# Band attention on one core: which engine multiplies the 384- and 512-column probability rows by their inverse sums

## The chip, the cores and the metric

The kernel runs on one core of a Trainium2 chip. The metric is the time of one execution on the device, in microseconds (us); lower is better. A core has a matrix engine (TensorE, in the profile PE, with its weight loads as PEld), three engines for elementwise work (VectorE or DVE, ScalarE or ACT, GpSimd or POOL), and DMA queues; SyncE (SP) issues most of the loads. Each engine works through its own queue in a fixed order, and waits at an instruction whose inputs or buffers are not ready.

## The reference, cut to what matters

The kernel computes a small encoder trunk of two layers on 512 tokens of width 1024, in float32. The first layer mixes tokens by a matrix memory (mLSTM), the second by attention over a band of chunks; both add an attention over 256 memory tokens, and each is followed by a gated channel mixer with a short convolution. The change lies in the band attention of the second layer:

```python
def band_attention(q, k_pad, v_pad, rel_table):
    # chunk c (64 tokens) attends to keys of chunks c-8..c; 12 heads of width 64
    ...
    bias = rel_table.astype(jnp.float32)[:, idx]
    scale = B_HEAD_DIM ** -0.5

    def one_chunk(c):
        ...
        s = jnp.einsum('bqhd,bkhd->bhqk', qc, kc).astype(jnp.float32) * scale + bias
        valid = (start - KV_PAD + kj) >= 0
        s = jnp.where(valid, s, -jnp.inf)
        p = jax.nn.softmax(s, axis=-1).astype(vc.dtype)
        return jnp.einsum('bhqk,bkhd->bqhd', p, vc)
```

With 512 tokens the band holds every earlier chunk, so that a block of 128 queries with number T (0 to 3) sees the first (T + 1) x 128 keys: 128, 256, 384 or 512 columns.

## The kernel before, in words

Activations lie with features on the 128 partitions and tokens along the columns. Float32 products are made from a high and a low part of each operand: the helper `split` (lines 146 to 151) casts the source to the high part on ScalarE (line 147) and subtracts it on VectorE to get the low part (line 148), and `mm3` (lines 203 to 205) adds three matmuls, high by high, high by low, low by high.

The second mixer goes over six pairs of heads (j = 0 to 5). `project_pair(j)` makes keys, values and queries of a pair with TensorE, eight steps of `mm3` a projection, and evacuates them on VectorE (lines 1480, 652) and ScalarE (`head_queries` and `head_keys`, lines 600 to 613). `band_attention(j, ...)` is the attention of the pair. Its generator `softmax(T)` does for both heads h of the pair:

- scores of 128 queries against (T + 1) x 128 keys on TensorE (line 622), into a PSUM bank of the group `sc` (three banks);
- line 1518, VectorE: adds the bias, negates, and keeps the row's smallest value `mn`; the result `e` goes to SBUF and frees the bank;
- line 1522, ScalarE: the exponential, with the row's sum `sm` as a second result (a short extra instruction reads it out);
- line 1523, VectorE: `sm` becomes its reciprocal;
- line 1524, VectorE: `e` is multiplied by `sm`, one scalar for each partition. This is the line that changes.

`transposed(T)` then turns `e` over on TensorE in blocks of 128 x 128 (line 1533, T + 1 blocks into one bank of the group `tr`, which has two), and `split` takes the bank to the high and the low probabilities in `pt` (ScalarE's cast 147, then VectorE's subtraction 148, which frees the bank). The program writes them in the order softmax 0, softmax 1, transposed 0, softmax 2, transposed 1, softmax 3, transposed 2, transposed 3; then the products with the values (lines 1554 and 1555) and their evacuation (`values`, lines 641 and 642). Rows of line 1524 are buffers of the group `t`, eight in all, and `sm` comes from a rotating set of small buffers.

What sets the order of the work: `weave` (lines 1566 to 1583) puts a fixed number of `mm3` steps of other work, projections of later pairs or parts of the output projection, behind each step of the attention, so that TensorE has matmuls while the elementwise engines work. In this stage no engine's order is written by hand: the framework that lays out the instructions takes the program's order as a priority and issues to each engine, by its own estimate of when inputs and buffers are ready, what comes first. The queues so made are fixed in the program. (In the channel mixers and at the beginning, the order of TensorE, ScalarE and VectorE is written by hand.) Weights come through SyncE's queue into three buffers `wr`, from which `split` makes `wh` and `wl`; the bias rows come through GpSimd's queue (line 1508).

The memory attention of the same mixer (line 679 for the exponential, 682 for the multiplication) has a code of its own and is not touched.

Of the kernel before, what the change touches and what calls it, by code (L numbers as in the profile page):

```python
# [12 lines left out]
AF = mybir.ActivationFunctionType  # L13
ALU = mybir.AluOpType
# [45 lines left out]
def trunk(  # L60
# [19 lines left out]
    V, A, G = nc.vector, nc.scalar, nc.gpsimd  # L80
# [14 lines left out]
    def sb(tag, shape, dtype=F32):  # L95
        count[0] += 1
        return pool.tile(shape, dtype, tag=tag, name=f"{tag}{count[0]}", bufs=bufs[tag])

    def ps(tag):
        count[0] += 1  # L100
        return psum.tile([P, S], F32, tag=tag, name=f"p{tag}{count[0]}", bufs=pbufs[tag])
# [6 lines left out]
    def small(n=4, dtype=F32):  # L108
        smalls[0] += 1
        i = smalls[0] % 26  # L110
        return sb("s0" if i < 6 else "s1" if i < 12 else "s2", [P, 16], dtype)[:, :n]
# [34 lines left out]
    def split(hi, lo, src, on_act=True, pinned=False):  # L146
        high = A.copy(hi, src) if on_act else V.tensor_copy(hi, src)  # L147
        low = V.tensor_tensor(out=lo, in0=src, in1=f(hi), op=ALU.subtract)  # L148
        if pinned:
            pin(high)  # L150
            pin(low)
# [485 lines left out]
    def values(outs):  # L637

        s, t = sb("t", [P, S]), sb("t", [P, S])
        for o, r in zip(outs, HEADS):  # L640
            A.copy(t[r, :], o[HD:, :])
            V.tensor_tensor(out=s[r, :], in0=o[:HD, :], in1=t[r, :], op=ALU.add)
        hi, lo = sb("u", [P, S], F32R), sb("u", [P, S], F32R)
        split(hi, lo, s)
        return hi, lo
# [9 lines left out]
    def scores(outs, q, tsl, k, c):  # L655

        for h in range(2):
            head_scores(outs[h], h, q, tsl, k, c, True)
# [537 lines left out]
    e, u, c, r = (cpool.tile([P, TT, AH], F32, name=f"gate{i}") for i in range(4))  # L1196
# [270 lines left out]
    def hi_at(pt, s, T, n=1):  # L1467
        return pt[:, s * 640 + (T + 1) * P : s * 640 + (T + 1 + n) * P]

    def lo_at(pt, s, T, n=1):  # L1470
        return pt[:, (3 - s) * 640 + (T - s) * P : (3 - s) * 640 + (T - s + n) * P]

    def blocks(pt, o, step, n):
        a = pt[:, o : o + P]
        return bass.AP(tensor=a.tensor, offset=a.offset, ap=[list(a.ap[0]), [step, n], [1, P]])
# [25 lines left out]
    def band_attention(j, q, k, v):  # L1501
        pts = [sb("pt", [P, 5 * S], F32R) for _ in range(2)]
        biases = []
        for h in range(2):
            rep = reps[2 * j + h]
            biases.append(sb("bias", [P, S]))
            src = bass.AP(tensor=rep.tensor, offset=rep.offset + P - 1, ap=[[RW - 1, P], [1, S]])
            tc.keep_in_program_order(G.dma_start(biases[h], src))
        es = {}

        def softmax(T):
            n = (T + 1) * P
            ss = [ps("sc")[:, :n] for _ in range(2)]
            scores(ss, q, slice(T * P, n), k, slice(0, n))
            for h in range(2):
                e = sb("t", [P, S])[:, :n]
                mn, sm = small(1), small(1)
                V.tensor_tensor_reduce(
                    out=e, in0=ss[h], in1=biases[h][:, S - n :], scale=-1.0, scalar=BIG,
                    op0=ALU.add, op1=ALU.min, accum_out=mn,  # L1520
                )
                A.activation(e, e, AF.Exp, bias=mn, scale=-1.0, accum_out=sm)
                V.reciprocal(sm, sm)
                V.tensor_scalar(e, e, sm, None, op0=ALU.mult)
                es[T, h] = e
            yield

        def transposed(T):
            n = (T + 1) * P
            for h in range(2):  # L1530
                tp = ps("tr")
                for b in range(T + 1):
                    nc.tensor.transpose(tp[:, b * P : (b + 1) * P], es[T, h][:, b * P : (b + 1) * P], ident)  # L1533
                split(
                    blocks(pts[h], (T + 1) * P, 640, T + 1), blocks(pts[h], 3 * 640 + T * P, -768, T + 1),
                    tp[:, :n].rearrange("p (b t) -> p b t", t=P),
                )
            yield

        yield from softmax(0)  # L1540
        yield from softmax(1)
        yield from transposed(0)
        yield from softmax(2)
        yield from transposed(1)
        yield from softmax(3)
        yield from transposed(2)
        yield from transposed(3)
        outs = []
        for h in range(2):
            o2 = ps("tr")  # L1550
            outs.append(o2)
            for s in range(TT):
                w = v[s][:, h, :]
                nc.tensor.matmul(o2[:, s * P :], w, hi_at(pts[h], s, s, TT - s), start=s == 0, stop=False)  # L1554
                nc.tensor.matmul(o2[:, s * P :], w, lo_at(pts[h], s, s, TT - s), start=False, stop=s == TT - 1)  # L1555
            yield
        mixes[j] = values(outs)
# [220 lines left out]
```

## Time and profile before

| | us |
|---|---|
| median of 3 runs | 1168.01 |
| lowest and highest | 1167.87 and 1168.32 |
| the profiled execution | 1168.55 |
| its span, first to last instruction | 1166.5 |
| granted TensorE clock, mean | 0.998 of full speed |

How to read the profile: busy times are of one execution, in us, and means of single instructions in ns. A row of a group names the line of the kernel, the engine, the operation, what it writes and reads (`t<-t,s` is from a row and a column of scalars to a row), the shapes, the count, the busy time and mean, and behind the second bar the engine's idle time just before such instructions with what ended it. "A <- B: 1.3, 4, 0.4" in the view of waits means that A waited for B 1.3 us in total, 4 times, 0.4 at the longest. A timeline row is start (us), duration (us), engine, line, operation; what stands in brackets is the idle time before it and what ended it. Matmuls are pipelined, and a matmul's row is longer than the distance to the next one.

### The profile page before, as it was taken

How to read it: one execution, taken by the hardware profiler on the slowest of the kernel's cores; microseconds unless marked ns; L12 is line 12 of the kernel's file. 1: busy time of each engine (PE TensorE's matmuls, PEld its weight loads, DVE VectorE, ACT ScalarE, POOL GpSimd, SP SyncE). 2: the span in 40 equal slices, each digit the busy share in tenths (PEclk: the TensorE clock that was granted, in tenths of full speed). 3: DMA queues.
4: the chain of work that ended last, by engine and by line, in shares of the span. 5: the costliest groups of instructions: out<-in, count | busy, mean ns of one | idle time of the engine just before them, and what ended most of it. 6: DMA issues, size and time to landing. Idle time of an engine off the chain costs nothing.

```text
span 1166.5 us, 19282 instructions
## 1 busy us (share of the span) xinstructions
PE 1156.2 (99%) x7189; PEld 1033.2 (89%) x7189; DVE 1001.8 (86%) x1781; ACT 747.9 (64%) x1343; POOL 151.2 (13%) x254
## 2 busy tenths in 40 slices
PE   9999999999999999999999999999999999999997
PEld 9988888888999999999888888778899999999986
DVE  6877688779999988888797888898999998889977
ACT  6548677657776655555575667776776665555654
POOL 1211101000122222111021000100010111111100
PEclk9999999999999999999999999999999999999999
DMA  8745325244468878777564322335445767777682
GB/s 282 230 110 134 96 56 153 66 134 140 139 157 182 213 178 195 182 173 162 147 193 133 91 62 63 122 107 157 142 126 143 174 146 180 172 180 174 143 157 78
DMA packets 207855, 171.26 MB, mean 147 GB/s; under 512 B 9256, under 2 KB 182030, under 8 KB 207762
## 3 DMA queue, kind: packets, MB, share of 16 engines
q1 hardware_dynamic: 188018, 123.93, 37.1%
q0 software_dynamic: 19168, 45.06, 19.3%
q8 instruction: 56, 0.92, 0.3%
q10 hardware_dynamic: 576, 1.05, 0.2%
q14 instruction: 37, 0.30, 0.1%
HBM read 133.09 MB, written 40.85 MB: 149 GB/s over the span
## 4 chain that ended last, share of the span: by engine, by line
PE 96%; DVE 2%; ACT 1%; DMA 0%; issue 0%; POOL 0%; POOLq 0%; DVEq 0%
PE pmm L203 19%; PE pmm L204 18%; PE pmm L205 18%; PE ptr L204 6%; PE ptr L203 6%; PE ptr L205 6%; PE psc L203 5%; PE psc L204 5%; PE psc L205 5%; PE psc L622 2%; PE ptr L1533 1%; PE ptr L1554 1%; PE ptr L1555 1%; PE ptr L691 1%; PE pmm L513 0%; PE ptr L705 0%
## 5 line engine op out<-in xcount | busy, mean ns | idle before, releaser
L203 PE MATMUL pmm<-u,wh 128*128 128x256 f32 (+1 forms) x992 | 334.9, 338 | 0.1
L205 PE MATMUL pmm<-u,wl 128*128 128x256 f32 (+1 forms) x992 | 332.1, 335 | 0.0
L204 PE MATMUL pmm<-u,wh 128*128 128x256 f32 (+1 forms) x992 | 331.9, 335 | 0.0
L148 DVE TENSOR_TENSOR wl<-wr,wh 128x1024 fp32r<-128x1024 f32 (+4 forms) x165 | 184.8, 1120 | 56.0 <-ACT wh L147 55.4
L205 PEld LDWEIGHTS pmm<-u,wl 128*128 128x128 f32 x992 | 186.3, 188 | 18.9
L203 PEld LDWEIGHTS pmm<-u,wh 128*128 128x128 f32 x992 | 186.4, 188 | 16.7 <-ACT u L147 0.9
L204 PEld LDWEIGHTS pmm<-u,wh 128*128 128x128 f32 x992 | 186.5, 188 | 16.2 <-DVE u L148 0.5
L147 ACT CAST wh<-wr 128x1024 fp32r<-128x1024 f32 (+4 forms) x165 | 159.6, 970 | 62.5 <-PE pmm L204 30.1
L203 PE MATMUL ptr<-u,wh 128*128 128x512 f32 x272 | 106.5, 392 | 0.0
L204 PE MATMUL ptr<-u,wh 128*128 128x512 f32 x272 | 106.3, 391 | 0.0
L205 PE MATMUL ptr<-u,wl 128*128 128x512 f32 x272 | 105.8, 389 | 0.0
L147 ACT CAST fh<-pt 128x512 fp32r<-128x512 f32 x120 | 74.8, 625 | 34.5 <-DVE pt L1059 33.2
L203 PE MATMUL pmm<-u,fh 128*128 128x256 f32 x320 | 88.8, 278 | 0.0
L205 PE MATMUL pmm<-u,fl 128*128 128x256 f32 x320 | 88.6, 277 | 0.0
L204 PE MATMUL pmm<-u,fh 128*128 128x256 f32 x320 | 88.5, 276 | 0.0
L981 ACT COPY t<-pmm 128x256 f32<-128x256 f32 x120 | 45.0, 375 | 67.3 <-PE pmm L205 67.2
L148 DVE TENSOR_TENSOR fl<-pt,fh 128x512 fp32r<-128x512 f32 x120 | 82.3, 687 | 3.1
L765 DVE SCALAR_TENSOR_TENSOR t<-t,cols,t 128x511 f32<-128x511 f32 x88 | 65.9, 749 | 7.3 <-ACT t L772 5.8
L203 PE MATMUL psc<-u,wh 128*128 128x256 f32 (+1 forms) x208 | 63.2, 304 | 0.0
L205 PE MATMUL psc<-u,wl 128*128 128x256 f32 (+1 forms) x208 | 62.9, 302 | 0.0
L204 PE MATMUL psc<-u,wh 128*128 128x256 f32 (+1 forms) x208 | 62.9, 302 | 0.0
L203 PEld LDWEIGHTS pmm<-u,fh 128*128 128x128 f32 x320 | 60.1, 188 | 2.2 <-ACT t L981 0.7
(359 smaller groups left out, 2642.0 us busy)
## 6 DMA issues: line engine op xcount, KB each, us to landing
wr<-in_ffn_w_up_dram SPq DMA_DIRECT2D x46, 512.0 KB, 8.5
pt<-in_ffn_w_up_dram SPq DMA_DIRECT2D x40, 512.0 KB, 8.3
wr<-in_ffn_w_down_dram SPq DMA_DIRECT2D x32, 512.0 KB, 5.4
wr<-in_a_w_in_dram SPq DMA_DIRECT2D x20, 512.0 KB, 3.8
xspill<-bias POOLq DMA_DIRECT2D x32, 256.0 KB, 7.0
without_row<-bias POOLq DMA_DIRECT2D x24, 256.0 KB, 4.1
wr<-in_w_kv_dram SPq DMA_DIRECT2D x12, 512.0 KB, 4.0
without_row<-t POOLq DMA_DIRECT2D x24, 256.0 KB, 4.1
```

The source lines that it names most:

```text
L147: high = A.copy(hi, src) if on_act else V.tensor_copy(hi, src)
L148: low = V.tensor_tensor(out=lo, in0=src, in1=f(hi), op=ALU.subtract)
L203: nc.tensor.matmul(o, lh, rh, start=first, stop=False, skip_group_check=more)
L204: nc.tensor.matmul(o, lh, rl, start=False, stop=False, skip_group_check=more)
L205: nc.tensor.matmul(o, ll, rh, start=False, stop=last, skip_group_check=more)
L622: nc.tensor.matmul(o, a, b, start=first and i == 0, stop=i == 1)
L691: nc.tensor.transpose(tp[:, a, i, :], es[T2, h][:, i, a * P : (a + 1) * P], ident)
L765: V.scalar_tensor_tensor(acc[:, n:], src[:, : S - n], self.fw[:, c * FT + j : c * FT + j + 1], acc[:, n:], op0=ALU.mult, op1=ALU.add,)
L981: A.copy(o, r[:, :H])
L1533: nc.tensor.transpose(tp[:, b * P : (b + 1) * P], es[T, h][:, b * P : (b + 1) * P], ident)
L1554: nc.tensor.matmul(o2[:, s * P :], w, hi_at(pts[h], s, s, TT - s), start=s == 0, stop=False)
L1555: nc.tensor.matmul(o2[:, s * P :], w, lo_at(pts[h], s, s, TT - s), start=False, stop=s == TT - 1)
```

## The change

The multiplication of line 1524 is done by ScalarE for query blocks 2 and 3 (rows of 384 and 512 columns), as a copy with a scale for each partition; blocks 0 and 1 stay on VectorE. That concerns 2 blocks x 2 heads x 6 pairs = 24 of the 48 instructions. Nothing else is edited.

```diff
                 A.activation(e, e, AF.Exp, bias=mn, scale=-1.0, accum_out=sm)
                 V.reciprocal(sm, sm)
-                V.tensor_scalar(e, e, sm, None, op0=ALU.mult)
+                if T < 2:
+                    V.tensor_scalar(e, e, sm, None, op0=ALU.mult)
+                else:
+                    A.activation(e, e, AF.Copy, scale=sm)
                 es[T, h] = e
             yield
```

## The prediction, on record before the changed kernel ran

> **What bounds the kernel now.** I read the page first, then the table of busy time by stretch for the six band heads, the waits of TensorE, the groups with shapes kept apart, and last the timeline of two heads. The page says which engine the time belongs to.
>
> ```profile
> span 1166.5 us, 19282 instructions
> PE 1156.2 (99%) x7189; PEld 1033.2 (89%) x7189; DVE 1001.8 (86%) x1781; ACT 747.9 (64%) x1343; POOL 151.2 (13%) x254
> PE 96%; DVE 2%; ACT 1%; DMA 0%; issue 0%; POOL 0%; POOLq 0%; DVEq 0%
> ```
>
> The chain that ended last is TensorE for 96% of the span, VectorE for 2%, ScalarE for 1%. The profiled execution took 1168.55 us, 2.05 us more than its span of 1166.5; the median of the runs, 1168.01, lies 0.54 us below it. I work out a change against the profiled execution and put it on the median. A difference under 0.2% (2.34 us) is about what a measurement of this kernel cannot tell from nothing.
>
> The changed line 1524 runs only in the band attention of the second mixer.
>
> ```profile
> L1524 DVE TENSOR_SCALAR t<-t,s x48: 280/382/602, 630.3 to 795.1; 128x128 f32<-128x128 f32 x12, 128x256 f32<-128x256 f32 x12, 128x384 f32<-128x384 f32 x12, 128x512 f32<-128x512 f32 x12
> ```
>
> Its 48 instructions (shortest, median and longest in ns; first and last start in us) start between 630.3 and 795.1 us, twelve of each width, in six bursts, one for each pair of heads ("head pair" below). This is the table by stretch for the six bursts (length; busy PE, weight loads, VectorE, ScalarE, GpSimd; clock; DMA), and behind it a stretch of the output projection, in which matmuls of 512 columns follow one another without a wait.
>
> ```profile
> 629.00:642.00 13.00, 12.89 (x72) 10.76 (x71) 11.74 (x42) 8.54 (x26) 2.19 (x4) 1.00 0.42 113
> ...
> 752.00:770.00 18.00, 17.67 (x95) 14.35 (x94) 16.69 (x51) 14.12 (x36) 1.09 (x2) 1.00 0.26 68
> ...
> sum 93.00, PE 92.56 PEld 76.61 DVE 82.42 ACT 65.86 POOL 6.62; mean PE 15.43 PEld 12.77 DVE 13.74 ACT 10.98 POOL 1.10
> 820.00:840.00 20.00, 20.00 (x90) 16.52 (x89) 19.61 (x35) 15.34 (x24) 1.08 (x2) 1.00 0.53 159
> ```
>
> In the 93.00 us of the bursts TensorE is idle for 0.44 us. VectorE is busy 82.42 us of them (89%), ScalarE 65.86 (71%). So there is little time to win, and VectorE is the nearer of the two helpers to holding TensorE up. Weight loads are busy for 76.61 of 93.00 us (82%); in the projection's stretch, where TensorE is never idle, they are at 16.52 of 20.00 (83%). The bursts are about as tightly packed as that stretch.
>
> The Trainium skill, page "Perfetto Trace Analysis", section "Identifying the Most-Contended Engine", holds matmul busy time for a bad measure, and tells the reader to judge headroom by weight-load busy time. By that rule alone 16.4 us of the bursts could still be won; the trace disagrees on the headroom, since a stretch without any wait shows the same share.
>
> The waits of TensorE and of its weight loads from 612 to 832 us give the ceiling of a gain (us in total, times, longest).
>
> ```profile
> PE psc L622 <- DVE s L1518: 0.3, 1, 0.3
> ...
> PEld ptr L1533 <- DVE pt L148: 1.3, 4, 0.4
> PEld ptr L1554 <- DVE pt L148: 1.0, 4, 0.3
> ...
> PEld psc L622 <- DVE s L1518: 0.6, 1, 0.6
> PEld ptr L705 <- DVE pt L148: 0.6, 3, 0.2
> ```
>
> The largest waits that VectorE ends are 1.3 (transposes of the rows, waiting for a bank that the subtraction of the split frees), 1.0 and 0.6 (products that wait for the low half), and 0.6 (scores that wait for a bank): 3.5 us. None names line 1524, and the view of that line lists nobody who waited for it.
>
> **The change part by part.** These are the groups of the exponential (1522) and of the multiplication that moves (1524), by shape, and the nearest thing to the new instruction: line 351, ScalarE's scaling by a column.
>
> ```profile
> L1522 ACT ACTIVATE t<-t,s 128x512 f32<-128x512 f32 x12 | 8.7, 724 | 3.3 <-DVE s L1518 3.3
> L1522 ACT ACTIVATE t<-t,s 128x384 f32<-128x384 f32 x12 | 7.4, 615 | 3.6 <-DVE s L1518 3.6
> L351 ACT ACTIVATE u<-fl,cols 128x512 fp32r<-128x512 f32 x4 | 2.9, 714 | 0.0
> L1524 DVE TENSOR_SCALAR t<-t,s 128x512 f32<-128x512 f32 x12 | 5.8, 481 | 0.1
> L1524 DVE TENSOR_SCALAR t<-t,s 128x384 f32<-128x384 f32 x12 | 5.2, 432 | 0.1
> ```
>
> *Removed from VectorE:* 12 x 0.481 + 12 x 0.432 = 10.96 us. In the bursts its load falls from 82.42 to 71.46 of 93.00 us (77%). *Added to ScalarE:* 0.714 us for 512 columns by line 351; for 384 I take off what the exponential loses between the shapes, 0.724 - 0.615 = 0.109, so 0.605 us. That is 12 x 0.714 + 12 x 0.605 = 15.83 us, and ScalarE rises from 65.86 to 81.69 us (88%). The two engines change places: the busier helper was at 89% and will be at 88%. Neither amount is on the path as such, because TensorE sets the end; what counts is the rows at which TensorE has to wait. No DMA is added or moved. The transfers that these engines release (weights after the split, the bias rows after line 1518) may start a little earlier or later; no wait of TensorE above names one, so I cost that at nothing.
>
> *What VectorE's relief is worth.* Here is the end of the first head pair.
>
> ```profile
> 640.08 0.84 ACT L147 CAST pt<-ptr 128x384 fp32r<-128x384 f32 x2
> 640.21 0.16 DVE L1523 RECIPROCAL s<-s 128x1 f32<-128x1 f32 x1 [0.28 <-ACT t L1522]
> 640.41 0.49 DVE L1524 TENSOR_SCALAR t<-t,s 128x512 f32<-128x512 f32 x1
> 640.81 1.01 DVE L148 TENSOR_TENSOR pt<-ptr,pt 128x384 fp32r<-128x384 f32 x2
> 641.41 0.88 PEld L1533 LDWEIGHTS ptr<-ident,t 128*128 128x128 f32 x8 [0.43 <-DVE pt L148]
> ```
>
> A moved multiplication of 0.49 us stands on VectorE right ahead of the subtractions whose end lets the transposes go on, 0.43 us late. With it gone the subtractions could start as soon as the cast ahead of them is done, and the 0.43 us is the most that this place gives. What is late next is that cast: if the new scaling of the other head goes ahead of it on ScalarE, the cast starts up to 0.71 us later and the gain is gone. For all such places the bounds are 0 and -3.5 us (the rows above); I take -0.4, this place alone, because it is the only one that I saw with a moved instruction directly in front.
>
> *What the longer row costs.* Each moved row becomes ready later by 0.714 - 0.481 = 0.233 us (512 columns) or 0.605 - 0.432 = 0.173 us (384), and by any time that ScalarE is not free. If nothing hid it, the sum would be 12 x 0.233 + 12 x 0.173 = 4.87 us. The cover is the time between a row's end and its first transpose. The tightest place I found is the last row of the second head pair.
>
> ```profile
> 665.75 1.06 ACT L147 CAST wh<-wr 128x1024 fp32r<-128x1024 f32 x1
> 666.08 0.15 DVE L1523 RECIPROCAL s<-s 128x1 f32<-128x1 f32 x1
> 666.60 0.48 DVE L1524 TENSOR_SCALAR t<-t,s 128x512 f32<-128x512 f32 x1
> 667.20 0.31 PEld L1533 LDWEIGHTS ptr<-ident,t 128*128 128x128 f32 x3 [0.33 <-PE ptr L1533]
> ```
>
> The reciprocal is done at 666.23, the row at 667.08, the transposes load at 667.20: a cover of 0.12 us. ScalarE is in a weight cast until 666.81, so the row would be done at 666.81 + 0.714 = 667.52, 0.44 us later than now, and TensorE would be late by 0.44 - 0.12 = 0.32 us. That is the price I take for rows whose cover is too short; the bounds are 0 and +4.87.
>
> *The new wait.* Before, the multiplication stood behind its reciprocal on one engine. Now ScalarE waits for VectorE's reciprocal, and behind that waiting instruction are queued the casts of the transposed blocks, the weight casts, and the exponentials of the next rows. The transposes wait for the casts through the two banks they use. ScalarE has waits already that such a one may sit inside:
>
> ```profile
> ACT wh L147 <- PE pmm L204: 13.7, 10, 3.2
> ACT t L1522 <- DVE s L1518: 12.5, 17, 1.9
> ACT pt L147 <- PE ptr L1533: 10.3, 17, 2.1
> ```
>
> That is 13.7 + 12.5 + 10.3 = 36.5 us of ScalarE's idle time in the whole stage, over twice the 15.83 us that it gets. This is the cover, and it is why I leave the rest at nothing.
>
> The sum: -0.4 + 0.32 = -0.08 us. From 1168.55 that makes 1168.47 for a profiled execution, and about 1167.9 for the median.
>
> **The rivals.** *VectorE's backlog was what held TensorE* (faster). For it: 89% in the bursts, and the 3.5 us of waits all end with VectorE. Against it: most of them end with the subtraction of a split, which itself waits for ScalarE's cast, and ScalarE gets fuller. To show, over 2.34 of the 3.5 us must go; with 2.8 gone (four fifths) the time is 1168.01 - 2.8 = 1165.2.
>
> *ScalarE's queue holds up the casts* (slower). The place is the end of a head pair: two exponentials of 512 columns, two new scalings and the casts of the rows before are on ScalarE together, and a scaling stands in front of a cast that frees a bank. It decides from 2.34/24 = 0.10 us per moved row that no cover takes; with no cover at all the time is 1168.01 + 4.87 = 1172.9. For it: the load of 88%, and the short cover in the second head pair. Against it: the 36.5 us of waits. The Trainium skill, page "ScalarE: Activation LUTs", section "Rules for kernel authors", says that plain multiplications belong on VectorE and not on ScalarE, and so speaks for this rival; the trace agrees on the single instruction, 714 ns against 481.
>
> *The order of the queues changes more than the costs.* No order is written by hand in this stage; the framework lays the queues out by its own estimates, and another engine for 24 instructions can shift where the transposes stand among the projections' matmuls. The bursts show what a worse order is worth: TensorE idles 0.33 us in the stretch from 752 to 770 and 0.11 in the first. All six like the worst would be 6 x 0.33 - 0.44 = +1.54 us, 1169.6; all idle time gone -0.44, 1167.6. Both lie within 0.2%.
>
> *The change does not do what it says*, for instance by a load of activation tables around each copy. Line 351 is the same operation with a column as its scale, and the whole stage has a single load, behind the last row:
>
> ```profile
> L283 ACT ACT_TABLE_LOAD  x1: 1283/1283/1283, 801.9 to 801.9; - x1
> ```
>
> I give it 1 in 100, inside "slower".
>
> **How the numbers follow.** No measurable change 0.62: my sum at -0.08 us, with the bounds from reordering inside it. Faster 0.16: the backlog rival, which needs two thirds of all waits and loses to a fuller ScalarE. Slower 0.22: larger than faster, because its bound of 4.87 us is wider than 3.5 and new waits have no ceiling in the rows. The forecast is 1167.9. The range has to keep 8 in 10: its lower end goes to the backlog rival's 1165.2, its upper end to two thirds of the uncovered price, 1168.01 + 3.25 = 1171.3; about 1 in 10 is left out on each side.
>
> **What would show it.** Right: in the changed profile line 1524 keeps 24 instructions on VectorE, and the new line has 24 on ScalarE at about 0.605 and 0.714 us; VectorE loses near 11 us and ScalarE gains near 16 over the span; TensorE's idle time in the six bursts stays below 2 us. Wrong toward faster: the waits of lines 1533, 1554 and 622 for VectorE shrink to under 1.2 us and the stage ends over 2 us sooner. Wrong toward slower: waits of the transposes for ScalarE (the new scaling, or the casts of line 147) appear with over 2 us in total. A shift of the stages outside 612 to 832 us would mean that I looked in the wrong place.

## The result, and the profile after

The changed kernel takes 1180.01 us (median of 4 runs, 1179.72 to 1180.40); the kernel before, run beside it, 1168.16. The ratio is 1.0101, with a 95% interval of 1.0085 to 1.0117: 11.85 us slower, where the forecast was 1167.9 and the upper end of its range 1171.3. In all that follows a loss is counted against the runs of the kernel before that were made beside that kernel; their median was 1168.16 to 1168.52.

First the page of the changed kernel: span, busy time by engine, chain of waits.

```profile
span 1178.0 us, 19285 instructions
...
PE 1159.9 (98%) x7189; PEld 1033.2 (88%) x7189; DVE 994.3 (84%) x1757; ACT 760.4 (65%) x1367; POOL 150.9 (13%) x254
...
PE 92%; DVE 3%; ACT 3%; DMA 1%; issue 1%; SPq 0%; POOL 0%; DVEq 0%; POOLq 0%; ACTq 0%
```

The span is 11.5 us longer, with the same 7189 matmuls. TensorE's share of the chain went from 96% to 92%, and what it lost stands mostly with VectorE, ScalarE and a DMA. The moved work itself is what it should be. This is the view of the new line 1527 (count; shortest, median, longest ns; first and last start; then who waited for it):

```profile
L1527 ACT ACTIVATE t<-t,s x24: 601/666/729, 637.4 to 798.1; 128x384 f32<-128x384 f32 x12, 128x512 f32<-128x512 f32 x12
...
  PEld ptr L1536: 0.9, 4
```

The transposes (1533 before, 1536 now: the change adds three lines) wait for it 0.9 us in all. That is not where 11.85 us went. The waits of TensorE from 612 to 840 us (total us, times, longest) say where:

```profile
PEld pmm L203 <- ACT wh L147: 5.2, 1, 5.2
PE pmm L203 <- DVE rb L298: 4.7, 1, 4.7
PEld pmm L205 <- DVE wl L148: 2.6, 1, 2.6
PEld ptr L1557 <- DVE pt L148: 2.2, 5, 0.6
PE pmm L205 <- DVE wl L148: 1.9, 1, 1.9
```

Two single waits, of 5.2 and 2.6 us on the weight side (4.7 and 1.9 are the same stops, seen by the matmuls), outweigh the rest. They belong to `mm3` (lines 203 to 205) and to the split of a *weight* (147, 148), not to the attention. The table by stretch puts them behind the last head pair; before, then after (length; busy PE, weight loads, VectorE, ScalarE, GpSimd; clock; DMA share; GB/s):

```profile
800.00:840.00 40.00, 40.00 (x178) 33.06 (x177) 37.68 (x61) 29.80 (x45) 4.33 (x8) 1.00 0.60 183
```

```profile
800.00:840.00 40.00, 32.87 (x138) 25.87 (x137) 29.01 (x44) 21.36 (x33) 4.33 (x8) 0.91 0.56 169
```

Before, TensorE has no idle time here; after, 7.13 us of it, and a clock of 0.91. TensorE, VectorE and ScalarE all do less in these 40 us, so none of them is the new bound: they wait for one another. The place is the end of the out-projection, `OutProjection.finish` (lines 728 to 741). Its first five column tiles were computed among the attention; three, numbers 5 to 7, are left, and their weights are still to be split. This is TensorE's timeline there, first before, then after (start, duration, operation; in brackets the idle time before it and what ended it):

```profile
808.57 0.39 PE L203 MATMUL pmm<-u,wh 128*128 128x512 f32 x1
808.80 0.39 PE L204 MATMUL pmm<-u,wh 128*128 128x512 f32 x1
809.02 0.39 PE L205 MATMUL pmm<-u,wl 128*128 128x512 f32 x1
809.25 0.39 PE L203 MATMUL pmm<-u,wh 128*128 128x512 f32 x1
```

```profile
811.19 0.47 PE L203 MATMUL pmm<-u,wh 128*128 128x512 f32 x1 [0.49 <-DVE fh L736]
811.50 0.40 PE L204 MATMUL pmm<-u,wh 128*128 128x512 f32 x1
811.79 0.47 PE L203 MATMUL pmm<-u,wh 128*128 128x512 f32 x1
812.10 0.40 PE L204 MATMUL pmm<-u,wh 128*128 128x512 f32 x1
817.23 0.80 PE L203 MATMUL pmm<-u,wh 128*128 128x512 f32 x1 [4.73 <-DVE rb L298]
817.82 0.63 PE L204 MATMUL pmm<-u,wh 128*128 128x512 f32 x1
820.35 0.79 PE L205 MATMUL pmm<-u,wl 128*128 128x512 f32 x1 [1.90 <-DVE wl L148]
820.94 0.63 PE L203 MATMUL pmm<-u,wh 128*128 128x512 f32 x1
```

The reader is to see the order. Before, column tile 5 goes high, high, low, and on. After, the first two products of tile 5, then of tile 6, then of tile 7 come first, and only then tile 5's product with the low weights (205). So TensorE cannot go on with tile 5 until the weights of tile 7 have been cast. These are VectorE's and ScalarE's rows of the same place after the change:

```profile
810.37 1.88 DVE L736 TENSOR_TENSOR fh<-fh,pmm 128x512 f32<-128x512 f32 x3
812.16 0.68 DVE L736 TENSOR_TENSOR fh<-fh,psc 128x512 f32<-128x512 f32 x1
...
818.41 0.75 DVE L352 SCALAR_TENSOR_TENSOR u<-fl,cols,u 128x512 fp32r<-128x512 f32 x1
819.08 3.49 DVE L148 TENSOR_TENSOR wl<-wr,wh 128x1024 fp32r<-128x1024 f32 x3
```

```profile
809.15 1.05 ACT L147 CAST wh<-wr 128x1024 fp32r<-128x1024 f32 x1 [0.98 <-PE pmm L204]
...
816.15 1.03 ACT L147 CAST wh<-wr 128x1024 fp32r<-128x1024 f32 x1
```

The third cast ends at 817.18, and TensorE's 4.73 us end at 817.23. (The timeline names VectorE's norm sum, line 298, as the releaser of that matmul; its weight load, in the list of waits, names the cast. In e10 below the two come apart: the cast ends at 814.18 and that norm sum at 814.90, and the same matmul starts at 814.24.) The three subtractions that make the low weights stand behind all five residual sums and the norm work, and the first lands after 820. Before, the first of them stood right behind the first sum:

```profile
806.05 0.69 DVE L736 TENSOR_TENSOR fh<-fh,pmm 128x512 f32<-128x512 f32 x1
806.65 1.22 DVE L148 TENSOR_TENSOR wl<-wr,wh 128x1024 fp32r<-128x1024 f32 x1
```

and the third cast was done at 812.18:

```profile
811.14 1.04 ACT L147 CAST wh<-wr 128x1024 fp32r<-128x1024 f32 x1
```

Nothing in the edited lines asks for that. Counted matmul by matmul (each against the one of the same number in the old trace), TensorE is 2.62 us behind the old trace at 811.19, 7.75 at 817.23, 10.42 at 820.35 and 11.93 at 823.45, and stays there. So 9.3 us are lost in 12 us of time: 5.1 at the cast, 2.3 at the low weights, and 1.9 in matmuls that run slowly after the stop. The order of SyncE's queue changed too. Before, then after:

```profile
798.35 0.37 SPq L864 DMA_DIRECT2D pt<-in_ffn_w_up_dram  x1
798.77 1.22 SPq L869 DMA_DIRECT2D pt<-in_ffn_w_up_dram  x2
804.13 0.37 SPq L162 DMA_DIRECT2D wr<-in_b_w_out_dram  x1
```

```profile
801.31 0.37 SPq L162 DMA_DIRECT2D wr<-in_b_w_out_dram  x1
801.87 0.44 SPq L864 DMA_DIRECT2D pt<-in_ffn_w_up_dram  x1
802.36 2.38 SPq L869 DMA_DIRECT2D pt<-in_ffn_w_up_dram  x2
```

The load for column tile 7 went ahead of the three loads of the channel mixer's up-projection, on which VectorE's line 1059 waits, and with it what is queued behind that line.

### The profile page after: what moved, and what is told of

It reads as the page before. It is cut to its first block, busy times and chain, and to the rows that moved or that the text cites. A ratio compares the mean times of both kernels' runs of the same rounds, so it can differ in the third digit from the quotient of the medians.

```text
span 1178.0 us, 19285 instructions
## 1 busy us (share of the span) xinstructions
PE 1159.9 (98%) x7189; PEld 1033.2 (88%) x7189; DVE 994.3 (84%) x1757; ACT 760.4 (65%) x1367; POOL 150.9 (13%) x254
## 4 chain that ended last, share of the span: by engine, by line
PE 92%; DVE 3%; ACT 3%; DMA 1%; issue 1%; SPq 0%; POOL 0%; DVEq 0%; POOLq 0%; ACTq 0%
PE pmm L203 18%; PE pmm L205 18%; PE pmm L204 18%; PE ptr L204 6%; PE ptr L203 6%; PE ptr L205 6%; PE psc L203 5%; PE psc L204 5%; PE psc L205 5%; PE psc L622 2%; PE ptr L1536 1%; ACT t L1522 1%; PE ptr L691 1%; PE ptr L1557 1%; PE ptr L1558 1%; DMA pt<-in_ffn_w_up_dram 1%
## 5 line engine op out<-in xcount | busy, mean ns | idle before, releaser
L148 DVE TENSOR_TENSOR u<-t,u 128x512 fp32r<-128x512 f32 x78 | 55.8, 719 | 9.0 <-ACT u L147 8.4
```

## The experiments

Theory: the framework, having other costs for 24 instructions, laid the queues out differently, and the new order at the finish costs the time. Rival: the moved work itself costs it, by ScalarE's queue or the longer rows. Eight of the twelve kernels have the program of one kernel and the order of another, written as dependencies that fix only the order within a queue (four lists: TensorE, ScalarE, VectorE, SyncE, from the second mixer to the finish). Fixing an order costs next to nothing by itself: from 620 to 808 us, where e10, e11 and e12 have the work and the order of the kernel before, TensorE moves by less than 0.1 us against it. The edit:

```diff
+    ins = {i.name: i for i in nc.cur_bb.bb.instructions}
+    for ids in ORDER:
+        for a, b in zip(ids, ids[1:]):
+            dep = mybir.DependencyInfo(mybir.DependencyClass.NoSync, mybir.DependencyReason.DATA)
+            tc.add_manual_dep(ins[f"I-{b}"], f"I-{a}", dep, reason="order")
```

The expectations call their theories A, B, A1 and so on, each for itself.

**e1_new_work_old_order.** The changed kernel, ORDER the four queues of the kernel before.

> The 24 multiplications are on ScalarE as in the changed kernel, but from the first place to the last at which the two kernels' queues differ, the queues of TensorE, ScalarE, VectorE and SyncE are fixed to the order of the kernel before (each moved instruction stands in ScalarE's queue where ScalarE was at the end of its reciprocal). Theory A (the framework's new order of the queues costs the time, above all at the end of the output projection, and the work that moved costs little): 1168 to 1171 us. Theory B (the work on ScalarE makes the rows and all behind them late, whatever the order): 1178 to 1181 us.

Measured: 1173.06 us, ratio 1.0039 (1.0024 to 1.0054), +4.5 us, which is above theory A's 1171: the work costs more than expected in an order not made for it. The loss at the finish is gone: TensorE is 4.7 us late when the attention ends and 4.8 at the end of the span. What remains was lost at the rows; since this trace is 0.9 us early at 620 us, before the first row, its rows lose 5.6 us. Both places that the prediction priced can be read here, since all else stands as it stood. The first head pair's transposes, which had waited 0.43 us at 641.41:

```profile
640.49 0.42 PEld L1536 LDWEIGHTS ptr<-ident,t 128*128 128x128 f32 x4 [0.39 <-DVE pt L148]
641.48 0.42 PEld L1536 LDWEIGHTS ptr<-ident,t 128*128 128x128 f32 x4 [0.57 <-DVE pt L148]
```

The 0.43 us was not saved but became 0.39 and 0.57, because two scalings now stand ahead of the casts on ScalarE. And the second head pair's last row:

```profile
667.02 0.72 ACT L1527 ACTIVATE t<-t,s 128x512 f32<-128x512 f32 x1
```

```profile
667.79 0.42 PEld L1536 LDWEIGHTS ptr<-ident,t 128*128 128x128 f32 x4 [1.24 <-ACT t L1527]
```

There the wait grew from 0.33 to 1.24 us: the scaling waits behind the weight cast, as foreseen, but that cast also ends 0.3 us later, having another scaling ahead of it.

**e2_old_work_new_order.** The kernel before, ORDER the four queues of the changed kernel.

> All 48 multiplications stay on VectorE, each moved one right behind its reciprocal, but the four queues are fixed to the order of the changed kernel. Theory A: 1177 to 1181 us, with TensorE waiting between 808 and 825 us as in the changed kernel. Theory B: 1167 to 1170 us.

Measured: 1180.70 us, 1.0106 (1.0091 to 1.0121), +12.2 us. The whole loss, without one moved instruction, and at the same matmuls:

```profile
817.83 0.79 PE L203 MATMUL pmm<-u,wh 128*128 128x512 f32 x1 [4.73 <-DVE rb L298]
...
820.95 0.80 PE L205 MATMUL pmm<-u,wl 128*128 128x512 f32 x1 [1.90 <-DVE wl L148]
```

So the order is enough, and the rival falls as the main cause.

**e3_pair_4_alone and e4_all_but_pair_4.** Which of the moved instructions turn the layout? Only the four of pair j = 4, or only the other 20:

```diff
-                if T < 2:
+                if T < 2 or j != 4:
```

```diff
-                if T < 2:
+                if T < 2 or j == 4:
```

> Only the fifth head pair (j = 4) scales its 384- and 512-column rows on ScalarE: 4 instructions of 24, and the framework plans freely. It gives the queues at the end of the output projection the same order as in the changed kernel. Theory A: 1176 to 1179 us (the loss at the end of the projection, without the small losses in the other pairs). Theory B: a sixth of the loss, 1170 us.

> The five other head pairs (20 of 24 instructions) scale on ScalarE, the fifth as before; the framework plans freely and gives the end of the output projection the order of the kernel before, but for two VectorE instructions. Theory A: 1168 to 1171 us. Theory B: five sixths of the loss, 1178 us.

Measured: 1178.50 us, 1.0083 (1.0066 to 1.0100), +10.0 us for four instructions; and 1169.42 us, 1.0007 (0.9998 to 1.0016), +0.9 us for the other 20, which is not told apart from nothing. In e3 TensorE has the new order at the finish, in e4 the old; ScalarE and VectorE follow, but for a few instructions. Twenty moved rows cost next to nothing, four cost 10 us: the loss does not grow with the work moved.

**e7_all_rows.** All 48 rows on ScalarE.

```diff
-                if T < 2:
+                if T < 0:
```

> All 48 multiplications go to ScalarE, those of 128 and 256 columns too, twice as many as in the change; the framework plans freely, and gives the end of the projection the order of the kernel before but for two VectorE instructions. Theory A: 1169 to 1174 us, faster than the change although more work moves. Theory B: 1182 us or more.

Measured: 1171.44 us, 1.0027 (1.0017 to 1.0036), +3.1 us. Twice the moved work is 8.7 us cheaper than the change, since with it TensorE's finish comes out in the old order.

**e5_old_load_order and e6_old_finish_order.** The changed kernel with half of the finish put back: in e5 SyncE's queue alone (the third weight load behind the three loads of the up-projection), in e6 TensorE, ScalarE and VectorE alone.

> The changed kernel with its queues fixed as they are, except SyncE's: the load of the third weight block of the output projection goes behind the three loads for the channel mixer again, as in the kernel before. Theory A1 (within A: that load in front of the others makes VectorE's first sums of the mixer late, and everything behind them): 1170 to 1173 us. Theory A2 (within A: the orders of TensorE, ScalarE and VectorE at the end of the projection, with the high products of three column tiles ahead of the first low part): 1176 to 1180 us.

> The changed kernel with its queues fixed as they are, but from the end of the attention to the first column tiles of the projection TensorE, ScalarE and VectorE go in the order of the kernel before (one VectorE subtraction excepted, which the early load needs); SyncE keeps the new order of loads. Theory A1: 1175 to 1180 us. Theory A2: 1169 to 1173 us, with the waits between 808 and 825 us gone.

Measured: 1178.51 us, 1.0089 (1.0072 to 1.0106), +10.2; and 1171.66 us, 1.0028 (1.0017 to 1.0039), +3.4. The late loads, which had looked like the cause in the trace (VectorE's chain starts 4.3 us later), are worth about 1.6 us by the medians, and the intervals of e5 and of the change overlap. The order of the three engines is worth 11.85 - 3.36 = 8.5.

**e8_split_first.** A repair in the program: the weights of column tile 5 are split ahead of the loop.

```diff
             norm = mixer.norm
+            ahead = {j: weights(rows(self.w, j * P, P), KT, P) for j in range(5, 6)}
             for j in range(KT):
-                o = self.o[j] if j in self.o else run(project(self.w, j * P, self.mixes))
+                o = self.o[j] if j in self.o else run(project(self.w, j * P, self.mixes, "mm", ahead.get(j)))
```

> The change, and in the program the weights of the projection's column tile 5 are loaded and split ahead of the loop over the column tiles, so that their low part has priority over the residual sums; the framework plans freely. Theory A: 1168 to 1172 us. Theory B: 1178 to 1180 us.

Measured: 1173.98 us, 1.0048 (1.0033 to 1.0063), +5.7 us. It takes away about half and misses what was expected: TensorE is 3.5 us late at 812, 5.5 at 821 and 6.0 at 856. From 808 us on the trace loses 4.2 us where the changed kernel's loses 10.0. The largest stop left, 1.6 us, waits for a residual sum, which now stands behind the split that was moved ahead, and the next is 1.0 us.

**e9_old_finish_and_loads.** Both repairs, e5 and e6 together.

> The changed kernel with both repairs at once: the order of TensorE, ScalarE and VectorE from the end of the out-projection on as before (as in e6), and SyncE's third weight load behind the three loads of the channel mixer's up-projection (as in e5). In e6 TensorE was 2.2 us late when the attention ended and 3.6 us late at 815 us. Theory A: those last 1.4 us are the loads', so 1171.7 - 1.4 = 1170.3 us, and only what the rows themselves cost remains (about 2.2 us over the kernel before). Rival: the order of the loads is worth nothing once the engines' order is restored: 1171.7. If the rest of e6's loss has nothing to do with rows, the time comes below 1169.3.

Measured: 1170.52 us, 1.0019 (1.0010 to 1.0029), +2.2 us, as theory A had it. The loads' share, 3.36 - 2.20 = 1.2 us, is a likely size and no more by the medians, since the two intervals overlap; the traces agree with it, with 2.0 us lost from 808 us on in e6 and 0.6 in e9.

**e10_new_finish_order, e11_new_finish_elementwise, e12_new_finish_tensor.** Now the other way round: the kernel before, with its own order everywhere except in the last 30 TensorE, 25 ScalarE and 35 VectorE instructions of the lists (e10), or in ScalarE's and VectorE's part alone (e11), or in TensorE's alone (e12). On TensorE the difference is four matmuls; on VectorE it is above all these:

```diff
 TensorE
 L203 MATMUL pmm_9268<-u_7365,wh_9264 128x512
 L204 MATMUL pmm_9268<-u_7366,wh_9264 128x512
+L203 MATMUL pmm_9326<-u_7365,wh_9322 128x512
+L204 MATMUL pmm_9326<-u_7366,wh_9322 128x512
+L203 MATMUL pmm_9366<-u_7365,wh_9362 128x512
+L204 MATMUL pmm_9366<-u_7366,wh_9362 128x512
 L205 MATMUL pmm_9268<-u_7365,wl_9265 128x512
...
 VectorE
 L736 TENSOR_TENSOR fh_8746<-fh_8746,pmm_8762 128x512
-L148 TENSOR_TENSOR wl_9265<-wr_9262,wh_9264 128x1024
 L736 TENSOR_TENSOR fh_8748<-fh_8748,pmm_8763 128x512
...
 L352 SCALAR_TENSOR_TENSOR u_9259<-fl_8754,cols_451,u_9258 128x512
+L148 TENSOR_TENSOR wl_9265<-wr_9262,wh_9264 128x1024
+L148 TENSOR_TENSOR wl_9323<-wr_9320,wh_9322 128x1024
+L148 TENSOR_TENSOR wl_9363<-wr_9360,wh_9362 128x1024
```

> The kernel before, with its work, its loads and its order everywhere, except that the last 30 matmuls, 25 ScalarE and 35 VectorE instructions at the end of the out-projection stand in the changed kernel's order. It is e6 turned round. Theory A (that stretch of the order alone does it): 1168.4 + 8.4 (what e6 took away) = 1176.8 us, up to 1178 with the slower clock, and a wait of TensorE of over 4 us near 812. Rival (the late rows or the late loads are needed for it to bite): under 1172.

> As e10, but only ScalarE and VectorE have the new order at the end of the out-projection; TensorE keeps the old one. Theory A1 (VectorE's order decides: the subtraction for the first tile's low weights stands behind all sums): the low weights come at about 806.05 + 9.9 = 816 us, TensorE, which wants them at 809.0, waits 7 us: 1168.4 + 7 = 1175.4 us, up to 1177 with the slower clock. Theory A2 (TensorE's order decides): under 1170.

> As e10, but only TensorE has the new order at the end of the out-projection: four matmuls of the second and third tile stand ahead of the first product with low weights; ScalarE and VectorE keep the old order. Theory A1 (VectorE's order decides): TensorE waits only for ScalarE's third weight cast, done at 812.2 us, so from 809.5 for 2.7 us: 1168.4 + 2.7 = 1171.1. Theory A2 (TensorE's order decides): 1176 or more.

Measured: e10 1177.44 us, 1.0078 (1.0063 to 1.0093), +9.1; e11 1178.64 us, 1.0085 (1.0068 to 1.0102), +10.3; e12 1173.97 us, 1.0046 (1.0031 to 1.0061), +5.7. TensorE's first stops at the finish, in e10, e11 and e12:

```profile
814.24 0.79 PE L203 MATMUL pmm<-u,wh 128*128 128x512 f32 x1 [4.69 <-ACT wh L147]
814.83 0.63 PE L204 MATMUL pmm<-u,wh 128*128 128x512 f32 x1
816.78 0.80 PE L205 MATMUL pmm<-u,wl 128*128 128x512 f32 x1 [1.33 <-DVE wl L148]
```

```profile
816.62 0.79 PE L205 MATMUL pmm<-u,wl 128*128 128x512 f32 x1 [7.69 <-DVE wl L148]
```

```profile
812.26 0.66 PE L203 MATMUL pmm<-u,wh 128*128 128x512 f32 x1 [2.48 <-ACT wh L147]
812.72 0.63 PE L204 MATMUL pmm<-u,wh 128*128 128x512 f32 x1
813.15 0.63 PE L205 MATMUL pmm<-u,wl 128*128 128x512 f32 x1
```

The stretch of the order is enough by itself, with no late row and no late load (e10). The elementwise engines' order is enough by itself too: with TensorE's old order the low weights come at 816.6 where they had been wanted at 809.0 (e11). TensorE's order alone costs less, since it then waits only for the third cast (e12). The two do not add: given the late subtractions, TensorE's new order does not hurt, and in the traces it fills part of the wait (9.8 us lost from 808 us on in e10, 10.8 in e11; the intervals of the medians overlap). The waits came out as worked out beforehand, 7 and 2.7 us against 7.69 and 2.48; both times came out about 3 us above, which the last section explains by the clock.

Counting matmul by matmul also tells rows and finish apart. This is what each trace loses against that of the kernel before (us); at 620 us, ahead of the rows, the traces already lie up to 1 us apart, and that is left out:

| | rows, 620 to 808 us | finish, 808 to 856 us |
|---|---|---|
| changed kernel | 1.8 | 10.0 |
| e1, new work, old order | 5.6 | 0.0 |
| e2, old work, new order | 2.0 | 11.4 |
| e3, pair 4 alone | 0.8 | 10.0 |
| e4, all but pair 4 | 1.5 | 0.2 |
| e5, old load order | 1.7 | 8.5 |
| e6, old finish order | 1.7 | 2.0 |
| e7, all rows | 2.9 | 0.4 |
| e8, split first | 1.7 | 4.2 |
| e9, both repairs | 1.7 | 0.6 |
| e10, new finish order | 0.1 | 9.8 |
| e11, its ScalarE and VectorE alone | 0.0 | 10.8 |
| e12, its TensorE alone | 0.0 | 4.5 |

So the 2.2 us that e9 leaves are mostly lost at the rows. They cannot be put down to the moved work alone: e2 loses as much there with nothing moved, and the same moved work costs 5.6 us in the old order and 1.7 or 1.8 in the order that the framework made for it.

What stays open: why the layout turns lies in the framework's estimates, which no trace shows. Pair 4's four instructions turn it (e3), but not with all 48 moved (e7). And the loss at the rows was not traced to single waits. None of these kernels is faster than the kernel before.

## Why the prediction was wrong

**The step that failed** is the rival "The order of the queues changes more than the costs". Its mechanism was named, with its reason, and then priced at -0.44 to +1.54 us from the idle time in the six bursts, which put it inside "no measurable change". The bound was taken where the changed instructions stand. But a list that is laid out anew can change as far as the layout reaches, and here it changed behind the last burst, right ahead of the stretch that the prediction itself had quoted as one without a wait (820 to 840 us). Measured: +9.1 us for that stretch of order alone (e10), 8.5 us taken away by putting it back (e6).

**"No DMA is added or moved."** No DMA is added, but one was moved past three others on SyncE's queue. It was costed at nothing; with the engines' order restored it is worth about 1.2 us by the medians, whose intervals overlap, and 1.4 in the traces (e6 and e9).

**Costs of single instructions**: right. 24 remained on VectorE and 24 went to ScalarE at 601 to 729 ns, against 0.605 and 0.714 us worked out. Over the span VectorE lost 7.5 us and ScalarE gained 12.5, less than the 11 and 16 of the forecast; neither mattered for the time.

**VectorE's relief**, -0.4: wrong. The wait at 641 became 0.39 and 0.57 (e1), and in the changed kernel too the two casts stand behind two scalings and end at 641.93 instead of 640.92. The prediction's own sentence on what is late next, the cast behind the scaling, is what happened, and it should have been the price.

**The longer row**, +0.32: right place, right mechanism, too small. There it cost 0.9 us in the old order (e1). For all rows together the medians give +0.9 to +4.5 us, depending on the order that they sit in (e4, e9, e7, e1), inside the bound of 0 to +4.87; e1's trace, with 5.6 us lost at the rows, is over it. So even with the finish unharmed the sum of -0.08 us was too low: e9 is slower by 2.2 us, and its interval excludes no change. That alone would have stayed under the upper end of the range, 1171.3; the finish took the time out of it.

**The 36.5 us of ScalarE's waits as cover**: right for the order that the framework made for the new work, where the weight loads of the transposes wait for the scaling 0.9 us in all. It is not right for any order: in the old one (e1) they wait 3.2 us.

**ScalarE's queue holds up the casts** was the rival on the right side, and the time went its way, but not by its mechanism: 1172.9 was its utmost, and e2 loses 12.2 us with no row moved to ScalarE.

**What would show it wrong** named the waits of the transposes as the place to look, or a shift outside 612 to 832 us. TensorE's idle time in the six bursts did stay below 2 us, as the prediction asked of being right: 93.00 - 92.21 = 0.79 us, in the same stretches. The loss stands at 811 to 824, inside the stage but on other lines; the table by stretch found it where the list of expected lines would not have.

## What to carry to other kernels

Where a framework orders the queues by its own cost estimates, an edit can turn the order elsewhere, so a forecast needs a term for that, and the place to look for its size is the tightest stretch that the layout reaches (here, where TensorE never waits because the low weights are done 1.2 us before they are wanted, 807.87 against 809.02), not the edited lines. Before explaining a surprise by the moved work, run the old work in the new order and the new work in the old: here the two runs gave 12.2 us for the order alone and 4.5 us for the work in the old order. They do not add up to 11.85, since the work has another price in each order, but they say which of the two to look at. Where a tuned stretch depends on an order, write that order down, so that a later edit is measured for what it does.

## What the hardware showed

In these traces a stop of TensorE of 2.48 us or longer cost more than its length. After it, matmuls of 512 columns start 0.43 us apart instead of 0.23, as in the rows of e12 above (812.72, 813.15), and the granted clock falls. A stop of 1.6 us in e8 left the clock at 1.00. These are the stretches of e12 and of e11:

```profile
812.00:816.00 4.00, 3.74 (x9) 2.94 (x10) 4.00 (x7) 1.97 (x4) 1.08 (x2) 0.57 0.51 170
816.00:820.00 4.00, 4.00 (x19) 3.30 (x18) 0.50 (x1) 0.55 (x1) 0.00 (x0) 1.00 0.48 133
```

```profile
816.00:820.00 4.00, 3.38 (x8) 2.70 (x9) 2.84 (x3) 0.00 (x0) 0.00 (x0) 0.50 0.49 142
820.00:824.00 4.00, 4.00 (x13) 3.16 (x13) 0.00 (x0) 0.00 (x0) 0.00 (x0) 0.68 0.86 251
```

In e12 the slow matmuls last from 812.3 to about 815.9 and add 1.6 us to a wait of 2.48 (2.79 us late at 812.26, 4.42 at 815.71); in e11 they last from 816.6 to 822.3 and add 2.8 to 7.69. That explains the expectation's miss in e11. In e12 the trace is 4.5 us late, which the wait and the slow matmuls make up; the median is 5.7 us above, but the profiled execution, 1173.03 us, is the fastest of four that reach 1174.59. In the traces' record of the granted clock it stands at half for 3.41 us in e12 (812.44 to 815.86), 6.83 in the changed kernel and 10.24 in e10 and e11: one, two and three times the same length. The Trainium skill, page "TensorE: Matmul & The Clock Gate", section "What's actually happening", has the clock drop to half after an idle window of about 3.4 us; here the drop came after a stop shorter than that, 2.88 us from one matmul's start to the next in e12, and the measurement decides.
